# FOX projections of heads 0 to 3 as three Strassen chunks

## The chip, the cores and the metric

One core of a Trainium2 chip runs the kernel; the other cores are idle. The metric is the time of one execution in device microseconds (us), as the median of several runs. A core has a matrix engine (TensorE, PE in the profile, with its weight loads as PEld), a vector engine (VectorE, DVE), an activation engine (ScalarE, ACT), a general engine (GpSimd, POOL) and a queue that only issues transfers (SyncE, SP). They run side by side and wait for each other through semaphores; each works through its own queue in order.

## The reference

One decoder block on 512 tokens of width 1024, all in float32:

```python
u = rmsnorm(x, norm_mix_g)
proj = u @ w_in                      # 1024 x 9240
(gq, gk, gv, gz, ga, gb, fq, fk, fv, ff, gate_a, gate_b) = split(proj)
# A: conv(4) + SiLU on gq, gk, gv; gated delta rule, 8 heads of 128; norm * silu(gz)
y_a = o_a @ w_proj_gdn
# B (FOX): per head rmsnorm of q and k, softmax(q k^T / sqrt(128) + c_t - c_s), causal, 8 heads of 128
y_b = o_b @ w_proj_fox
h = x + (sigmoid(gate_a) * y_a + sigmoid(gate_b) * y_b) @ w_out
x = h + square(relu(rmsnorm(h, norm_mlp_g) @ w_up)) @ w_down
```

The change concerns `fq, fk, fv` of heads 0 to 3: twelve blocks of 128 columns of `w_in`, 1536 columns in all, multiplied by u (512 x 1024).

## The kernel before

**A product in three terms.** Matrices are split into a rounded part and a remainder (`hi`, `lo`). A product is hi·hi + lo·hi + hi·lo, so each 128 x 128 weight block costs three matmuls. The split is one ScalarE cast (hi) and one VectorE subtraction (lo); for weights that is `prefetch_split` (L256, L257), for activations `split` (L286, L287).

**Weights come in units.** The list `seq` names every unit of weights (128 x 1024, 512 KB) in the order of use. `unit(name)` takes the next one and, ahead of it, splits two further units (`LA_SPLIT`) and loads three (`LA_RAW`). There are four buffers for hi and four for lo (`whl`), three for raw weights (`wraw`) and two more for the first factor of a Strassen chunk (`swp`). SyncE issues plain loads (L210, L227). Since the planner (below) may run ahead, how early a unit is really loaded or split depends on these buffers.

**Strassen chunks.** `stream` computes 512 columns of a projection as a 2 x 2 block product with seven instead of eight half-sized products (the Winograd form): P1 to P7, each with its own weight unit and its own form of u. For P1, P2 and P3 a quarter of the weights is loaded as it is; the units of P5, P6, P4 and P7 are made in place, by a DMA that GpSimd issues and that adds another quarter onto the raw tile of an earlier product (L219): P1 → P5 → P6 → P4 and P3 → P7. Such a DMA must wait until the earlier unit has been split. Each product is 24 matmuls of 256 columns (L1011). P1, P6, P7 and P4 of a chunk follow each other in one PSUM bank (U), with an eviction after each (copies on ScalarE L991, additions and subtractions on VectorE L993); P5 and P3 share a second bank (V), P2 has a third (W). In all there are three such banks (`NMM`). Before the change, `STREAM` holds seven chunks: FOX heads 4 to 7 (three chunks) and the two gates (four).

**Forms of u.** P1, P2 and P4 use u itself. `factors_u` makes the others (P5, P7, P6, P3): in two parts it reloads the normalised x from DRAM (L432), scales it (L436), forms sums of half-width blocks (L448, two instructions a form) and splits the result (L286, L287). They stay in 16 pages until the stream ends.

**Pages.** Most activations live in 128 x 512 float32 pages, 53 in all (`NPG`). An instruction whose result has no free page cannot be placed.

**Order of the work.** The main program issues dense products; besides them run generators (`tasks`): one step of each at every `tick()`. The stages: norm of x and gates; z projections 0 to 4; `gdn_group(0)` with the 12 projections of delta-rule heads 0 to 3 (L275 to L279) and their head work; `fox_pair(0)` and `fox_pair(1)`, the FOX projections of heads 0 to 3 (L961 to L964), with `factors_u` started between them; z projections 5 to 7; `gdn_group(1)`; the stream of seven chunks; the output projections; the MLP in Strassen form (L1171). Generators beside them: `group_chain` (triangular inversion `invert`, then `scan` over four chunks of tokens), one and later two `fox_worker`s (attention of one head at a time, as soon as `fq` holds its q and k, and its v), `decays` (decay tables; those of group 1 start when group 0's chain has ended). In `invert`, 31 elimination steps of two VectorE instructions each give way to other tasks whenever their estimated work passes `INV_STEP[g]`.

**Planner.** The program is compiled with `schedule_with_timeline_sim=True`: a planner orders each engine's instructions by a simulated timeline and lets an instruction pass ahead of one whose inputs or buffers are not ready. The order of issue in the code is thus a priority, not the final order; the final order is fixed before the kernel runs.

**The old FOX stage.** `fox_pair` computes, for each of three panels and four token blocks, 256 columns with 24 matmuls (8 of uhi and 8 of ulo against the weights' hi, 8 of uhi against their lo): 2 x 3 x 4 x 24 = 576 matmuls.

Of the kernel before, what the change touches and what calls it, by code (L numbers as in the profile page):

```python
# [39 lines left out]
LA_SPLIT = 2  # L40
INV_STEP = (2500, 900)


def hybrid_block(tc, a, out):
# [106 lines left out]
    seq = [("w_ab", 0)] + [("w_z", i) for i in range(NZ1)]  # L151
    seq += [("w_gdn", i) for i in range(12)] + [("w_fox", i) for i in range(12)]
    seq += [("w_z", i) for i in range(NZ1, H)] + [("w_gdn", 12 + i) for i in range(12)]
# [46 lines left out]
    def load(n):  # L200
        nme, i = seq[n]
        if nme in FACTOR:
            w, c, s_ = i
            q, old = FACTOR[nme]
            if old is None:
                if w == "w_st":
                    raw = (swp if nme == "P1" else wraw).tile([P, D], F32, tag="raw", name=nm("sraw"))
                else:
                    raw = fresh[2 if nme == "P2" else s_].tile([P, D], F32, tag="raw", name=nm("draw"))
                nc.sync.dma_start(raw, a[w][c, q, s_])  # L210
            elif (nme, i) in LONE:
                if n not in begun:
                    begin(n)
                raw = begun[n]
                nc.gpsimd.dma_start(raw, a[w][c, 2, s_], accum_op=ALU.add)
            else:
                raw = factors[old, i]
                assert seq.index((old, i)) < len(units)
                nc.gpsimd.dma_start(raw, a[w][c, q, s_], accum_op=ALU.add)  # L219
            factors[nme, i] = raw  # L220
            raws[n] = raw, [slice(0, D)]
            return
        w = 256 if nme == "w_ab" else D
        raw = wraw.tile([P, D], F32, tag="raw", name=nm("raw"))
        cuts = [slice(0, 512), slice(512, D)] if 0 < n < 3 else [slice(0, w)]
        for c in cuts:
            nc.sync.dma_start(raw[:, c], a[nme][i][:, c])  # L227
        raws[n] = raw, cuts
# [6 lines left out]
    def prefetch_new(n):  # L235

        for m in range(pos[0], min(len(seq), n)):
            if fresh and m not in raws and seq[m][0] in FACTOR and FACTOR[seq[m][0]][1] is None and seq[m][1][0] != "w_st":
                load(m)
            if seq[m] in LONE and m not in begun:  # L240
                begin(m)
# [39 lines left out]

    def split(src, scale=None, dst=None):

        hi, lo = dst or (page(F32R, "hi")[:, :], page(F32R, "lo")[:, :])
        if scale is None:
            act.copy(hi, src)  # L286
            vec.tensor_tensor(lo, src, hi.bitcast(F32), op=ALU.subtract)  # L287
        else:
            act.activation(hi, src, AF.Copy, scale=scale)
            vec.scalar_tensor_tensor(lo, src, scale, hi.bitcast(F32),  # L290
                                     op0=ALU.mult, op1=ALU.subtract)
        return hi, lo
# [133 lines left out]
    def factors_u():  # L426
        lo, hi = slice(0, 256), slice(256, 512)
        for part in range(2):
# [9 lines left out]
            for p in ("P5", "P7", "P6", "P3"):  # L438
                yield
                x = s1 if p == "P5" else s2  # L440
                for f in range(2):
# [5 lines left out]
                                    "P3": (c[k + 4][:, lo], s2[:, o], ALU.add)}[p]  # L447
                    vec.tensor_tensor(x[:, o], in0, in1, op=op)  # L448
                xh_, xl_ = split(x)
                for f in range(2):  # L450
# [387 lines left out]

    def gdn_group(g, box):
        AT = atp.tile([P, NI, P], F32, tag="AT", name=nm("AT"))  # L840
        hd = drp.tile([5, NCH, P, G, P], F32, tag=f"hd{g}", name=f"hd{g}")
        hts = []
        for i in range(G):
            h = g * G + i
            ys = []
            for j in range(3):
                ys.append(project(h, j))
                tick()
            hts.append(start(head(h, AT, *ys, box, hd)))
        return start(group_chain(g, AT, hd, hts))  # L850

# [97 lines left out]

    def fox_pair(hp):  # L950
        vts = ([], [])
        for pn in range(3):
            us = [unit("w_fox"), unit("w_fox")]
            pg2 = [page(s="fqk"), page(s="fqk")]
            for t2 in range(2):
                ps = mmps("fx")
                for tb in (2 * t2, 2 * t2 + 1):
                    o = ps[:, (tb % 2) * 256:(tb % 2 + 1) * 256]
                    for k in range(KT):
                        w = us[k // 4][0][:, (k % 4) * 256:(k % 4 + 1) * 256]  # L960
                        mm(o, uhi[k][:, cs(tb)], w, start=(k == 0), stop=False)  # L961
                        mm(o, ulo[k][:, cs(tb)], w, start=False, stop=False)  # L962
                    for k in range(KT):
                        mm(o, uhi[k][:, cs(tb)], us[k // 4][1][:, (k % 4) * 256:(k % 4 + 1) * 256], start=False,  # L964
                           stop=(k == KT - 1))
                    if tb % 2 == 0:
                        tick()
                if pn < 2:
                    act.copy(pg2[t2], ps)
                else:  # L970
                    for j in range(2):
                        (vec.tensor_copy if j else act.copy)(
                            v3(pg2[j][:, 2 * t2 * P:(2 * t2 + 2) * P], 2), v3(ps[:, :], 2)[:, :, cs(j)])
                tick()
            if pn < 2:
                fq.append((2 * hp + pn, pg2, vts[pn]))
            else:
                for v, x in zip(vts, pg2):
                    v += [x[:, cs(c)] for c in range(NCH)]

    def stream(parts, other):

# [11 lines left out]

        for p, c in STREAM:
            if p is None:
# [16 lines left out]
            done = parts[c][2]  # L1013
            at[0] = c
            if p == "P1":
# [74 lines left out]
    fws = [start(fox_worker())]  # L1090
    ch0 = gdn_group(0, box)
    fox_pair(0)
    fu = start(factors_u())
    fox_pair(1)
    start(decays(1, box, ch0))
# [4 lines left out]
    hold[0] = False  # L1100
    finish(fu)
    fws += [start(fox_worker()) for _ in range(1, NFW)]
# [38 lines left out]
    parts += [gate_chunk(i, to) for to in (sga, mg) for i in range(2)]  # L1141
    stream(parts, merge_gdn)

# [296 lines left out]
def _layout(inputs):  # L1440
# [20 lines left out]
    fx = w[:, 4112:7184].reshape(D, 3, H, P)  # L1461
    pan = []
    for hp in range(2):
        for h in (2 * hp, 2 * hp + 1):
            pan.append(np.concatenate([fx[:, 0, h], fx[:, 1, h]], axis=1))
        pan.append(np.concatenate([fx[:, 2, 2 * hp], fx[:, 2, 2 * hp + 1]], axis=1))
    o["w_fox"] = c(np.stack(pan).reshape(6, 2, 4, P, 256).transpose(0, 1, 3, 2, 4).reshape(12, P, D))
    q, k, v = [[fx[:, j, h] for h in range(H)] for j in range(3)]
# [3 lines left out]

    st = np.stack(st).reshape(7, 2, 4, P, 2, 256)
    o["w_st"] = c(np.stack([st[:, j, :, :, l] for j, l in ((0, 0), (0, 1), (1, 1), (1, 0))], 1)
                  .transpose(0, 1, 3, 2, 4).reshape(7, 4, 1, P, D))
    o["w_z"] = units(w[:, 3072:4096])
# [43 lines left out]
```

## Time and profile before

| | |
|---|---|
| median of 3 runs | 983.23 us (983.08 to 983.75) |
| span of the profiled execution (first to last instruction) | 980.2 us |
| around the span (median less span) | 3.0 us |
| TensorE busy | 970.8 us, 6545 matmuls |
| VectorE / ScalarE / GpSimd busy | 710.9 / 605.0 / 240.2 us |
| first and last old FOX matmul | 122.4 and 213.2 us |
| first and last matmul of the stream (L1011) | 324.7 and 543.5 us |
| the chain that ended last | PE 92%, DVE 4%, DMA 2% |

The profiled execution has no time of its own other than its span; the 3.0 us lie around it. A page of the profile shows for each engine the time in which it was busy, the span cut into 40 equal slices, the chain of work that ended last and the costliest groups of instructions. A group's row ends with its busy time, the mean duration of one (ns), and the idle time of its engine just before, with what ended it. Matmuls are pipelined: the duration of one record is longer than the distance to the next.

### The profile page before, as it was taken

The numbers are of one execution on the slowest core, as the hardware profiler recorded it, in microseconds if no ns is written. First come the engines' busy times: TensorE is split into PE (matmuls) and PEld (weight loads), VectorE is DVE, ScalarE is ACT, GpSimd is POOL, SyncE is SP. The second block draws the span as 40 slices with busy tenths as digits, with TensorE's granted clock in tenths as the row PEclk, the third lists the DMA queues.
The fourth block names the chain that finished last, engine by engine and source line by source line (L and its number), as shares of the span: only waits on it lengthen the run. The fifth ranks groups of instructions, "written<-read, shape, count | busy, mean of one in ns | idle before, by whom it ended". The sixth has DMA issues, their size and how long they took to land.

```text
span 980.2 us, 17198 instructions
## 1 busy us (share of the span) xinstructions
PE 970.8 (99%) x6545; PEld 874.8 (89%) x6545; DVE 710.9 (73%) x1204; ACT 605.0 (62%) x1050; POOL 240.2 (25%) x236
## 2 busy tenths in 40 slices
PE   8999999999999999999999999999999999999998
PEld 6788899998888999999999888889989989988986
DVE  6877778566577789855656535889896697698596
ACT  7766444766564787867656422678755765666761
POOL 1544120202533513522320005312121121121110
PEclk9999999999999999999999999999999999999999
DMA  7647662475437885757887735688798888889884
GB/s 266 213 135 223 174 158 90 130 239 181 129 116 228 189 166 141 197 129 166 236 201 215 273 103 171 125 181 173 190 188 196 187 173 206 181 175 202 186 166 119
DMA packets 93442, 174.38 MB, mean 178 GB/s; under 512 B 8016, under 2 KB 49200, under 8 KB 93360
## 3 DMA queue, kind: packets, MB, share of 16 engines
q1 hardware_dynamic: 78928, 120.85, 38.8%
q0 software_dynamic: 14432, 52.44, 30.5%
q8 instruction: 51, 0.84, 0.4%
q14 instruction: 31, 0.25, 0.1%
HBM read 152.25 MB, written 21.02 MB: 177 GB/s over the span
## 4 chain that ended last, share of the span: by engine, by line
PE 92%; DVE 4%; DMA 2%; ACT 1%; issue 1%; SPq 0%; DVEq 0%
PE mlp L1171 36%; PE st L1011 12%; PE mm L279 8%; PE mm L276 8%; PE mm L275 8%; PE fx L964 2%; PE fx L961 2%; PE fx L962 2%; PE fo L944 2%; PE sc L919 1%; PE pT L935 1%; DVE lo L257 1%; PE kk L639 1%; PE kq L647 1%; DMA ux<-ud 1%; PE v L797 1%
## 5 line engine op out<-in xcount | busy, mean ns | idle before, releaser
L1402 ACT CAST hi<-draw 128x1024 fp32r<-128x1024 f32 x124 | 130.0, 1050 | 118.4 <-PE mlp L1171 100.4
L1409 DVE TENSOR_TENSOR lo<-draw,hi 128x1024 fp32r<-128x1024 f32 x124 | 151.3, 1222 | 44.8 <-ACT hi L1402 41.6
L256 ACT CAST hi<-raw 128x1024 fp32r<-128x1024 f32 (+1 forms) x62 | 62.9, 1021 | 82.6 <-PE mm L276 59.5
L1171 PE MATMUL mlp<-hi,shi 128*128 128x512 f32 x280 | 109.5, 391 | 0.1
L1171 PE MATMUL mlp<-hi,slo 128*128 128x512 f32 x280 | 109.1, 390 | 0.0
L1171 PE MATMUL mlp<-lo,shi 128*128 128x512 f32 x280 | 109.0, 389 | 0.0
L257 DVE TENSOR_TENSOR lo<-raw,hi 128x1024 fp32r<-128x1024 f32 (+1 forms) x62 | 73.9, 1197 | 29.1 <-ACT hi L256 13.4
L1171 PE MATMUL mlp<-shi,lo 128*128 128x256 f32 x448 | 90.3, 283 | 0.0
L1171 PE MATMUL mlp<-slo,hi 128*128 128x256 f32 x448 | 90.3, 283 | 0.0
L1171 PE MATMUL mlp<-shi,hi 128*128 128x256 f32 x448 | 90.3, 283 | 0.0
L276 PE MATMUL mm<-ulo,hi 128*128 128x512 f32 x216 | 85.0, 394 | 1.2 <-DVE ulo L290 1.2
L275 PE MATMUL mm<-uhi,hi 128*128 128x512 f32 x216 | 85.0, 395 | 0.0
L257 DVE TENSOR_TENSOR lo<-sraw,hi 128x1024 fp32r<-128x1024 f32 x49 | 60.7, 1240 | 20.9 <-ACT hi L256 20.1
L1171 PEld LDWEIGHTS mlp<-shi,hi 128*128 128x128 f32 x448 | 70.6, 192 | 0.9
L1171 PEld LDWEIGHTS mlp<-shi,lo 128*128 128x128 f32 x448 | 69.9, 192 | 0.0
L1171 PEld LDWEIGHTS mlp<-slo,hi 128*128 128x128 f32 x448 | 69.8, 192 | 0.0
L256 ACT CAST hi<-sraw 128x1024 fp32r<-128x1024 f32 x49 | 51.3, 1047 | 26.6 <-PE st L1011 16.2
L1171 PEld LDWEIGHTS mlp<-hi,shi 128*128 128x128 f32 x280 | 52.6, 188 | 11.1 <-issue 0.7
L1171 PEld LDWEIGHTS mlp<-lo,shi 128*128 128x128 f32 x280 | 52.6, 188 | 11.1
L1171 PEld LDWEIGHTS mlp<-hi,slo 128*128 128x128 f32 x280 | 52.6, 188 | 10.3
L219 POOL DMA_DIRECT2D draw<-w_d x30 | 26.3, 876 | 129.9 <-DVE lo L1409 120.8
L219 POOL DMA_DIRECT2D draw<-w_u x32 | 27.7, 866 | 122.6 <-DVE lo L1409 120.0
(336 smaller groups left out, 2466.6 us busy)
## 6 DMA issues: line engine op xcount, KB each, us to landing
draw<-w_u POOLq DMA_DIRECT2D x32, 512.0 KB, 5.7
draw<-w_d POOLq DMA_DIRECT2D x32, 512.0 KB, 6.5
sraw<-w_st POOLq DMA_DIRECT2D x28, 512.0 KB, 5.9
draw<-w_d SPq DMA_DIRECT2D x26, 512.0 KB, 4.4
raw<-w_gdn SPq DMA_DIRECT2D x24, 512.0 KB, 3.8
draw<-w_u SPq DMA_DIRECT2D x24, 512.0 KB, 4.4
sraw<-w_st SPq DMA_DIRECT2D x21, 512.0 KB, 5.5
hd<-hd SPq DMA_DIRECT2D x34, 256.0 KB, 5.4
```

Source lines behind the costliest of these rows:

```text
L219: nc.gpsimd.dma_start(raw, a[w][c, q, s_], accum_op=ALU.add)
L256: act.copy(hi[:, c], raw[:, c])
L257: vec.tensor_tensor(lo[:, c], raw[:, c], hi[:, c].bitcast(F32), op=ALU.subtract)
L275: mm(o, w, rhi(k), start=(k == 0), stop=False)
L276: mm(o, w, rlo(k), start=False, stop=False)
L279: mm(o, lo[:, k * cols:(k + 1) * cols], rhi(k), start=False, stop=(k == KT - 1))
L944: mm(po[:, cs(i)], vt[c], st[i][:, cs(c)], start=(c == 0), stop=(c == i))
L961: mm(o, uhi[k][:, cs(tb)], w, start=(k == 0), stop=False)
L1011: mm(o, u, w, start=first and t == 0 and k == 0 and j == 0 and x is hi, stop=x is lo and k == 3, skip_group_check=True)
L1171: return (lambda *args, **kw: tc.keep_in_program_order(f(*args, **kw))) if self.pinned[0] else f
L1402: pact.copy(hi, raws[m][0])
L1409: pvec.tensor_tensor(lo, raws[m][0], hi[:, :].bitcast(F32), op=ALU.subtract)
```

## The change

Heads 0 to 3 get the form that heads 4 to 7 have. `fox_pair` and its 12 units `w_fox` go; three Strassen chunks come in their place, with 21 units `w_sf` in an order of their own (`EARLY`), computed by the same `stream`, which now takes the order as an argument. Chunk 0 holds v0, v1, q0, k0; chunk 1 q2, k2, q1, k1; chunk 2 q3, k3, v2, v3. Since the products need all forms of u, `factors_u` now starts inside `gdn_group(0)`, after the projections of its second head, and is finished before the stream begins. Its sums, and the lo parts of its splits, are made by GpSimd instead of VectorE. `INV_STEP` for group 0 falls from 2500 to 1300.

```diff
-INV_STEP = (2500, 900)
+INV_STEP = (1300, 900)
...
-    seq += [("w_gdn", i) for i in range(12)] + [("w_fox", i) for i in range(12)]
+    seq += [("w_gdn", i) for i in range(12)]
+    EARLY = [("P1", 0), ("P2", 0), ("P1", 1), ("P2", 1), ("P5", 0), ("P3", 0), ("P6", 0), ("P5", 1), ("P7", 0), ("P4", 0),
+             ("P3", 1), ("P6", 1), ("P1", 2), ("P2", 2), ("P7", 1), ("P5", 2), ("P4", 1), ("P3", 2), ("P6", 2), ("P7", 2),
+             ("P4", 2)]
+    seq += [(p, ("w_sf", c, 0)) for p, c in EARLY]
...
-                if w == "w_st":
+                if w in ("w_st", "w_sf"):
                     raw = (swp if nme == "P1" else wraw).tile([P, D], F32, tag="raw", name=nm("sraw"))
...
-    def split(src, scale=None, dst=None):
+    def split(src, scale=None, dst=None, lo_by=None):
...
             act.copy(hi, src)
-            vec.tensor_tensor(lo, src, hi.bitcast(F32), op=ALU.subtract)
+            (lo_by or vec).tensor_tensor(lo, src, hi.bitcast(F32), op=ALU.subtract)
...
-                    vec.tensor_tensor(x[:, o], in0, in1, op=op)
-                xh_, xl_ = split(x)
+                    pool.tensor_tensor(x[:, o], in0, in1, op=op)
+                xh_, xl_ = split(x, lo_by=pool)
...
-    def gdn_group(g, box):
+    def gdn_group(g, box, between=None):
...
             hts.append(start(head(h, AT, *ys, box, hd)))
+            if between and i in between:
+                between[i]()
...
-    def fox_pair(hp):
...
-    def stream(parts, other):
+    def stream(parts, order, other=None):
...
-        for p, c in STREAM:
+        for p, c in order:
...
-            at[0] = c
+            if other:
+                at[0] = c
...
-    ch0 = gdn_group(0, box)
-    fox_pair(0)
-    fu = start(factors_u())
-    fox_pair(1)
+    fu = []
+    ch0 = gdn_group(0, box, {1: lambda: fu.append(start(factors_u()))})
+    finish(*fu)
+    v01, v23 = ([], []), ([], [])
+    stream([fox_chunk((None, v01), (0, v01[0])), fox_chunk((2, v23[0]), (1, v01[1])), fox_chunk((3, v23[1]), (None, v23))],
+           EARLY)
     start(decays(1, box, ch0))
...
     ch1 = gdn_group(1, box)
     hold[0] = False
-    finish(fu)
...
-    stream(parts, merge_gdn)
+    stream(parts, STREAM, merge_gdn)
```

On the host side the quarters of `w_sf` are laid out as those of `w_st` are.

More of the change, by code (lines that the diff above doesn't have):

```diff
@@ L237, in prefetch_new @@
         for m in range(pos[0], min(len(seq), n)):
-            if fresh and m not in raws and seq[m][0] in FACTOR and FACTOR[seq[m][0]][1] is None and seq[m][1][0] != "w_st":
+            if fresh and m not in raws and seq[m][0] in FACTOR and FACTOR[seq[m][0]][1] is None and seq[m][1][0] not in ("w_st", "w_sf"):
                 load(m)
@@ L948, in fox_worker @@
             stores.append(start(store_late(obd[h], o)))
-    def fox_pair(hp):
[L951 to L979, printed above, removed]
-    def stream(parts, other):
+    def stream(parts, order, other=None):
         bank = {}
@@ L1461, in _layout @@
     fx = w[:, 4112:7184].reshape(D, 3, H, P)
[L1462 to L1467, printed above, removed]
     q, k, v = [[fx[:, j, h] for h in range(H)] for j in range(3)]
@@ L1471, in _layout @@
     st += [w[:, n + T * i:n + T * i + T] for n in (7192, 8216) for i in range(2)]
-    st = np.stack(st).reshape(7, 2, 4, P, 2, 256)
-    o["w_st"] = c(np.stack([st[:, j, :, :, l] for j, l in ((0, 0), (0, 1), (1, 1), (1, 0))], 1)
-                  .transpose(0, 1, 3, 2, 4).reshape(7, 4, 1, P, D))
+    sf = [np.concatenate(b, axis=1) for b in
+          ((v[0], v[1], q[0], k[0]), (q[2], k[2], q[1], k[1]), (q[3], k[3], v[2], v[3]))]
+    for name, m in (("w_sf", sf), ("w_st", st)):
+        m = np.stack(m).reshape(len(m), 2, 4, P, 2, 256)
+        o[name] = c(np.stack([m[:, j, :, :, l] for j, l in ((0, 0), (0, 1), (1, 1), (1, 0))], 1)
+                    .transpose(0, 1, 3, 2, 4).reshape(len(m), 4, 1, P, D))
     o["w_z"] = units(w[:, 3072:4096])
```

## The prediction

> **What bounds the kernel now.** I read the profile page first: totals, the slices and the granted clock.
>
> ```profile
> span 980.2 us, 17198 instructions
> ...
> PE 970.8 (99%) x6545; PEld 874.8 (89%) x6545; DVE 710.9 (73%) x1204; ACT 605.0 (62%) x1050; POOL 240.2 (25%) x236
> ...
> PE   8999999999999999999999999999999999999998
> ...
> PEclk9999999999999999999999999999999999999999
> ```
>
> TensorE is busy in every slice at full clock. Next I asked the waits for TensorE alone: is that busy time work, or work stretched by stalls?
>
> ```profile
> PE mm L276 <- DVE ulo L290: 1.2, 2, 0.7
> ...
> PE Q L741 <- ACT AT L725: 0.5, 1, 0.5
> ...
> PE pT L935 <- DVE p L932: 0.2, 1, 0.2
> ```
>
> The first is the largest, the last the smallest of nine kinds; they are 5.5 us together. So no other engine sets the end. Time leaves this kernel if TensorE has fewer matmuls to issue, and comes back if something makes TensorE wait.
>
> The busy time by stretches shows what other engines have to spare. The first row is the projections of delta-rule heads 0 to 3, the second the FOX projections that are replaced, the third the first part of the existing Strassen stream.
>
> ```profile
> 43.00:122.00 79.00, 77.79 (x385) 64.60 (x384) 63.29 (x127) 47.26 (x103) 26.45 (x22) 1.00 0.60 174
> ...
> 122.40:213.40 91.00, 90.52 (x926) 88.63 (x925) 60.00 (x147) 52.10 (x104) 14.26 (x13) 1.00 0.51 151
> 324.70:420.00 95.30, 95.13 (x818) 91.93 (x818) 81.58 (x196) 75.73 (x161) 37.21 (x35) 1.00 0.77 176
> ```
>
> After the length: busy time of PE, PEld, DVE, ACT, POOL; then clock, DMA share, GB/s. The third row matters most: there a Strassen stream already runs beside a delta-rule inversion, with DVE at 86%, ACT at 79% and DMA at 0.77, and TensorE still lost only 0.17 us of 95.3.
>
> **Part 1: fewer matmuls.** The groups of TensorE by line and their timeline (several merged into a row):
>
> ```profile
> L961 PE MATMUL fx<-hi,uhi 128*128 128x256 f32 x192 | 48.5, 288 | 0.0
> L962 PE MATMUL fx<-hi,ulo 128*128 128x256 f32 x192 | 47.8, 284 | 0.0
> ...
> L964 PE MATMUL fx<-lo,uhi 128*128 128x256 f32 x192 | 28.4, 285 | 0.0
> ```
> ```profile
> 124.28 1.12 PE L964 MATMUL fx<-lo,uhi 128*128 128x256 f32 x8
> ...
> 342.79 0.64 PE L1011 MATMUL st<-lo,hi 128*128 128x256 f32 x4
> ...
> 346.68 1.06 PE L647 MATMUL kq<-conv,conv 128*128 128x128 f32 x8
> 347.57 0.60 PE L919 MATMUL sc<-fk,fq 128*128 128x256 f32 x2
> 347.82 0.59 PE L1011 MATMUL st<-lo,hi 128*128 128x256 f32 x2
> ```
>
> Removed: 3 x 192 = 576 matmuls of 256 columns. Added: 3 chunks x 7 products x 2 halves x 12 = 504 of the same shape. The existing stream confirms the count: its own matmuls, alone, are these.
>
> ```profile
> 324.70:543.60 218.90, 156.87 (x1176) 145.81 (x1175) 1.00 0.75 184
> ```
>
> 1176 / 7 chunks = 168 a chunk, and 3 x 168 = 504. So 72 fewer. One record lasts 285 ns, but they overlap: eight take 1.12 us, so (1.12 - 0.28) / 7 = 0.120 us from one to the next; four of the stream take 0.64, again (0.64 - 0.28) / 3 = 0.120. The saving is 72 x 0.120 = **8.6 us**, not 72 x 0.285 = 20.5. All other matmuls stay; the stage shrinks from 91.0 to about 82.4 us, and a unit of weights (24 matmuls) lasts 2.9 us of pure stream, or 82.4 / 21 = 3.9 us with the other tasks' matmuls between.
>
> **Part 2: the weights.** 12 units become 21: 9 plain loads by SyncE, 12 adding DMAs by GpSimd, each onto the raw tile that the unit before it in its chain has just been split from. Rows of the replaced stretch, and one eviction of the stream (L993):
>
> ```profile
> L257 DVE TENSOR_TENSOR lo<-raw,hi 128x1024 fp32r<-128x1024 f32 x12 | 14.5, 1218 | 6.1 <-PE fx L964 4.1 <-ACT hi L256 1.3 <-issue 0.8
> ...
> L287 DVE TENSOR_TENSOR lo<-ux,hi 128x512 fp32r<-128x512 f32 x4 | 3.6, 896 | 1.8 <-ACT hi L286 1.8
> ...
> L448 DVE TENSOR_TENSOR ux<-ux,ux 128x256 f32<-128x256 f32 x6 | 2.3, 423 | 0.1
> ...
> L448 DVE TENSOR_TENSOR ux<-ux 128x256 f32<-128x256 f32 x2 | 1.2, 633 | 0.0
> ```
> ```profile
> L993 DVE TENSOR_TENSOR fqk<-fqk,st 128x512 f32<-128x512 f32 x9 | 6.1, 676 | 1.8 <-ACT fqk L991 1.8
> ```
> ```profile
> L256 ACT CAST hi<-raw 128x1024 fp32r<-128x1024 f32 x11 | 11.3, 1049 | 14.7 <-PE fx L962 14.7
> L436 ACT ACTIVATE ux<-ux,c_norm_mix_g 128x512 f32<-128x512 f32 x8 | 5.5, 723 | 2.7 <-DMA ux<-ud 2.6
> L969 ACT COPY fqk<-fx 128x512 f32<-128x512 f32 x8 | 4.6, 580 | 3.3 <-PE fx L964 3.3
> ```
>
> DVE in the stage: 60.0, plus 9 splits x 1.22 = 11.0, plus 9 subtracting or adding evictions x 0.68 = 6.1, less the sums of u that leave (3.6 + 2.3 + 1.2): 70.0 of 82.4 us, 85%. ACT: 52.1 + 9 x 1.05 + 4 more copies x 0.58 - 5.5 for u's scalings = 58.4, 71%. Both are below the third stretch's 86% and 79%, where TensorE did not wait. DMA, from the queues' rows and the landings:
>
> ```profile
> q1 hardware_dynamic: 78928, 120.85, 38.8%
> q0 software_dynamic: 14432, 52.44, 30.5%
> ```
> ```profile
> sraw<-w_st POOLq DMA_DIRECT2D x28, 512.0 KB, 5.9
> ```
> ```profile
> DMA to landing us min/median/max: 3.4/5.7/10.4
> ```
>
> A 512 KB (0.524 MB) adding transfer occupies the 16 engines for 0.305 x 980.2 x 0.524 / 52.44 = 2.99 us, a plain one for 0.388 x 980.2 x 0.524 / 120.85 = 1.65. The stage has 0.51 x 91 = 46.4 us; plus 12 x 2.99, less 3 x 1.65, less the reloads of u (8 half-sized, 6.6) gives 70.7 of 82.4, a share of 0.86 against 0.77: the one resource above its precedent. A link of a chain is a split (1.05 + 1.22) and a landing (5.9): 8.2 us. Split buffers are four, so unit n can be split once unit n-4 is used. In the new order the tightest links are two units long (P5 to P6 of chunk 0; P6 to P4 and P3 to P7 of chunk 2): P5 is split from 2.9 us on, P6 is then ready at 2.9 + 2.3 + 5.9 + 2.3 = 13.4 us, and wanted at 6 x 2.88 = 17.3. Spare 3.9 us; with the longest landing, 10.4, it would be 0.6 late. Cost taken: nothing, hidden behind the four units between; without that cover up to 0.6 us plus what DVE has queued ahead, at three links. GpSimd's queue gets 12 issues, each waiting for DVE's lo; behind one stand the FOX normalisations and the delta-rule output scaling, whose own results go to pages that the stream does not read.
>
> **Part 3: banks handed over without a unit between.** Products 6, 7 and 4 share one PSUM bank, and each must wait until the one before is evicted. In the new order P7 and P4 of chunk 0, and P6, P7, P4 of chunk 2, stand next to each other; the existing order always puts a unit between. From both sides: 0 each if the planner fills in other work (346.68 to 347.82 above shows it running kq and sc inside a unit), or a tail of 0.16, an eviction of 0.68 and one split ahead of it, 1.22: 2.1 each, 6.2 in all. Another chunk's unit, or the z projection behind, is ready at each place, so I take **1.0**, near the lower end.
>
> **Part 4: sums of u by GpSimd, earlier.** 16 sums of 128x256 and 8 differences of 128x512, with their 8 reloads, 8 scalings and 8 casts, move into the second half of the first group. The nearest GpSimd rows of these shapes:
>
> ```profile
> L1229 POOL TENSOR_TENSOR m<-gate,gate 128x256 f32<-128x256 f32 x16 | 19.6, 1241 | 83.2 <-DVE gate L1227 83.2
> ...
> L573 POOL TENSOR_TENSOR gu<-upper,ghi 128x512 fp32r<-128x512 f32 x8 | 9.4, 1176 | 12.0 <-ACT ghi L507 12.0
> ```
>
> 19.6 + 9.4 = 29.0 us, so GpSimd goes from 26.5 to 55.5 of 79. Their casts on ACT, and DVE's differences as they are now (min/median/max):
>
> ```profile
> L286 ACT CAST hi<-ux x8: 603/618/622, 193.0 to 237.5; 128x512 fp32r<-128x512 f32 x8
> L287 DVE TENSOR_TENSOR lo<-ux,hi x8: 681/688/1528, 193.6 to 238.2; 128x512 fp32r<-128x512 f32 x8
> ```
>
> In series a form takes 2 x 1.24 + 0.62 + 1.18 = 4.3 us, eight 34 us. From the middle of the group (82.5), with 5.5 for a reload and 2.9 for scalings: 125; with half of GpSimd's own 26.5 us between them, 138. The last form (P3) is wanted by unit 5, at 122.4 + 14.4 + some 3 us of other matmuls = 140. Just in time, so I charge nothing; each us beyond is a us of TensorE idle.
>
> GpSimd and DVE do hold each other up in this trace:
>
> ```profile
> 193.60 1.53 DVE L287 TENSOR_TENSOR lo<-ux,hi 128x512 fp32r<-128x512 f32 x1 [1.12 <-ACT hi L286]
> ```
> ```profile
> 192.54 2.04 POOL L889 TENSOR_TENSOR fqk<-fqk,fss 128x512 f32<-128x512 f32 x2
> 194.53 1.09 POOL L878 TENSOR_SCALAR_AFFINE_SELECT nd<-row 128x512 f32<-128x512 f32 x1
> ```
>
> The difference took 1.53 us instead of the median 0.69, with GpSimd's two multiplications from 192.54 to 194.58 beside it: it began 1.06 us after them, and its end, 195.13, comes 0.55 after theirs. If GpSimd's 29 us were all added to DVE, it would have 63.3 + 29 = 92 us of work in 79. But in that half of the group DVE has only 6 or 7 such two-input instructions of size, the weight splits; each waiting one GpSimd instruction of 1.2 makes 8 us, against 79 - 63.3 = 15.7 idle in the whole group, some 8 in this half. TensorE meanwhile has two more projection banks to fill, each 24 matmuls, by this row (1.98 - 0.39) / 7 = 0.227 us apart, 5.5 us:
>
> ```profile
> 50.24 1.98 PE L279 MATMUL mm<-uhi,lo 128*128 128x512 f32 x8
> ```
>
> Cost taken 0; bound 1.5 (one GpSimd instruction and some).
>
> [...]
>
> **Part 5: inversion steps.** By the code's count the 31 steps give way 9 times instead of 5, and the stage ticks 21 times, not 24, so group 0's chain ends 7 ticks later against group 1, and the decay tables with it. Heads 4 and 5 wait for theirs; the group's chain starts only after head 7, which has its table some 9 ticks early. Cost 0; if that cover went, one projection, 5.5 us, at most.
>
> **Sum.** 980.2 - 8.6 + 1.0 = 972.6 us of span. The run's median is 983.2, 3.0 more than the span; kept, that gives **975.6**. Its own range: 973.5 (no handover cost, the 0.5 wait at L741 gone, 0.6 for parts that this cannot see) to 978.5.
>
> **Rivals.** (a) *The weights come late.* For: DMA at 0.86, links of two units. Three links late by 0.6 + 1.2, or 5.4 us: **981.0**. Against: 85% of DVE has a precedent without waits, and several units are split ahead. (b) *GpSimd and DVE hold each other up; slower than before.* The place is the wait of unit 4 or 5 on the forms, its price the lateness one to one; it decides from 8.6 - 1.0 = 7.6 us on, and is measurably slower from about 9.6. If the two engines' lock stretches GpSimd's 29 us by half, 14.5 us, the last form is at 152, 12 late: **987.6**. (Seen from DVE, 92 - 79 = 13 us: nearly the same.) For: the 256-wide row of GpSimd, 1.24, is longer than the 512-wide one, 1.18, so it was stretched by something. Against: it takes half of GpSimd's other work ahead of the sums, and both parts strictly in series. [...] (c) *Pages run out.* u's 16 factor pages are taken from about 100 us on instead of from 193 to 238. In the new stage I count 32 for u and forms, 8 to 12 for FOX results, 5 of head 3, 5 of the inversion, 3 of the worker: 53 to 57 of 53. A chunk that cannot be evicted stops TensorE until pages return. Stopped for half of a chunk, 3.5 units x 3.9 = 14 us: **989.6**. Against: the third stretch holds the 32 and 12 too, with a head's and an inversion's pages and two workers', and shows 95.13 of 95.30. (d) *The change does nothing*, since something else sets the end: **983**. Against: 5.5 us of waits in 980.
>
> **Chances.** Forecast 0.68; (a) 0.14, of which 0.05 lands within 0.2%; (b) 0.09 (0.02 faster, 0.02 same, 0.05 slower); (c) 0.06 (0.01, 0.01, 0.04); (d) 0.03, same. Faster 0.68 + 0.09 + 0.02 + 0.01 = 0.80; same 0.11; slower 0.09. 0.2% (2.0 us) is about what a measurement of this kernel can tell from no change. The range runs from 973.5 to 982.0, through (a) and the 6.2 us handover bound; outside lie most of (b) and (c).
>
> **What would show it.** Right: the stream's line with 1680 matmuls at the same 0.12 us spacing, TensorE's busy time and span both lower by about 8 us, the total of its waits still below 8. (a) shows as TensorE waiting for lo splits whose casts wait for adding DMAs; (b) as one wait early in the stage on a GpSimd lo; (c) as TensorE waiting for evictions that sit idle themselves. Wrong altogether: a span that stays although 72 matmuls are gone.

## The result, and the profile after

The changed kernel takes **1009.46 us** (median of 4 runs, 1006.91 to 1010.19) against 983.37 for the kernel before (4 runs, 983.08 to 983.75) on the same chip: a ratio of 1.026, 95% interval 1.0242 to 1.0279. It is 26 us slower where 8 us less were forecast. The profiled run took 1010.19 us, 1.7 more than its span.

The page of the kernel after: totals, slices and granted clock.

```profile
span 1008.5 us, 17125 instructions
...
PE 974.1 (97%) x6473; PEld 873.6 (87%) x6473; DVE 720.2 (71%) x1194; ACT 616.8 (61%) x1061; POOL 274.3 (27%) x272
...
PE   8999979899999599999999999999999999999998
...
PEclk9999999999999799999999999999999999999999
```

The matmuls fell by 72, from 6545 to 6473, and yet TensorE is busy for 3.3 us more. There are new holes in its slices and one in its clock, all before 355 us. Next, the busy time by stretches, cut at the first matmul of the new stage and at the start of the later stream; first the kernel before, then the kernel after (length; busy PE, PEld, DVE, ACT, POOL; clock, DMA share, GB/s):

```profile
122.40:324.70 202.30, 201.82 (x1525) 183.25 (x1524) 135.75 (x299) 116.38 (x236) 53.37 (x46) 1.00 0.53 158
324.70:980.30 655.60, 651.05 (x4457) 595.17 (x4455) 479.75 (x732) 408.77 (x661) 144.96 (x146) 1.00 0.76 180
```
```profile
122.75:346.60 223.85, 200.84 (x1452) 179.77 (x1452) 141.47 (x288) 121.08 (x235) 69.50 (x65) 0.96 0.58 155
346.60:1008.60 662.00, 655.61 (x4456) 597.88 (x4456) 483.19 (x738) 409.88 (x663) 146.39 (x148) 0.99 0.76 178
```

Up to 122 us next to nothing is lost (0.35 us). In the next stretch TensorE has 73 matmul records fewer and needs 21.6 us more; it idles 23.0 us of it instead of 0.5. The rest, the same work in both, is 6.4 us longer. So the loss lies around the new stage and the second delta-rule group, and it is waiting. The waits of TensorE in the kernel after (us in total, times, longest):

```profile
PE st L986 <- DVE conv L603: 13.7, 3, 10.2
PE st L986 <- ACT fqk L966: 2.9, 3, 1.1
PE Qp L711 <- DVE Xd L693: 2.6, 1, 2.6
PE st L986 <- DVE fqk L968: 1.3, 3, 0.8
```

The timeline of the kernel after shows where they lie (start, duration, then in brackets the idle time before and what ended it). Two undisturbed rows of the stream stand on top.

```profile
123.77 0.64 PE L986 MATMUL st<-lo,uhi 128*128 128x256 f32 x4
124.25 0.64 PE L986 MATMUL st<-hi,uhi 128*128 128x256 f32 x4
...
132.72 0.71 PE L986 MATMUL st<-hi,uhi 128*128 128x256 f32 x4 [3.11 <-DVE conv L603]
...
142.80 0.71 PE L986 MATMUL st<-hi,uhi 128*128 128x256 f32 x4 [0.38 <-DVE fqk L968]
...
146.69 0.74 PE L986 MATMUL st<-hi,hi 128*128 128x256 f32 x4 [0.78 <-DVE fqk L968]
...
150.97 0.75 PE L986 MATMUL st<-hi,hi 128*128 128x256 f32 x4 [1.15 <-ACT fqk L966]
...
155.25 0.74 PE L986 MATMUL st<-hi,hi 128*128 128x256 f32 x4 [1.15 <-ACT fqk L966]
...
196.72 1.20 PE L711 MATMUL Qp<-Xd,AT 32*32 32x32 f32 x64 [2.56 <-DVE Xd L693]
...
346.64 1.19 PE L986 MATMUL st<-hi,uhi 128*128 128x256 f32 x4 [10.16 <-DVE conv L603]
```

Four matmuls every 0.48 us: 0.120 each, as forecast. Most of what is new are three larger waits (3.1, 2.6 and 10.2 us) and four handovers. A second cost is the **granted clock**. In the kernel before it was full in every slice; these are stretches of the kernel after, and two rows of the stream out of the first:

```profile
134.00:137.00 3.00, 3.00 (x16) 3.00 (x15) 0.96 (x5) 0.57 (x1) 2.09 (x3) 0.50 0.61 74
199.00:202.00 3.00, 3.00 (x16) 3.00 (x16) 0.16 (x1) 2.92 (x6) 0.00 (x0) 0.50 0.87 248
271.00:273.50 2.50, 2.50 (x13) 2.50 (x12) 2.01 (x3) 1.76 (x3) 2.50 (x3) 0.50 0.31 92
348.00:351.00 3.00, 3.00 (x16) 3.00 (x15) 2.96 (x8) 1.36 (x3) 0.39 (x1) 0.50 0.86 147
```
```profile
135.34 1.05 PE L986 MATMUL st<-hi,ulo 128*128 128x256 f32 x4
136.20 1.05 PE L986 MATMUL st<-lo,uhi 128*128 128x256 f32 x4
```

Four matmuls of the stream take 0.86 us at clock 0.50 (135.34 to 136.20), 0.48 at full clock: 44% of such a stretch is lost. In the trace the clock is halved in 133.9 to 137.3, 198.7 to 202.2, 270.4 to 273.8 and 338.7 to 352.3 us. The first three follow shortly on waits and are 3.4, 3.5 and 3.4 us long; the fourth begins in the wait of 10.2 us and is 13.6 long. TensorE works in 3.4, 3.5, 3.4 and (after its wait ends at 346.6) 5.7 us of them, 16 us in all, and 44% of it is about 7 us lost, an estimate (the matmuls of 270.4 to 273.8 are of other sizes). The last section sets the waits before them beside these lengths.

The account of the span: 72 x 0.120 = 8.6 us less work; waits of all kinds 24.6 more (30.1 against 5.5, adding up the waits of TensorE); clock about 7; sum 23 of the 28.3 us. The other 5 I can't assign.

### The profile page after: what moved, and what is told of

It is laid out like the page before. It is cut to its first block, busy times and chain, and to the rows that moved or that the text cites. A ratio compares the mean times of both kernels' runs of the same rounds, so it can differ in the third digit from the quotient of the medians.

```text
span 1008.5 us, 17125 instructions
## 1 busy us (share of the span) xinstructions
PE 974.1 (97%) x6473; PEld 873.6 (87%) x6473; DVE 720.2 (71%) x1194; ACT 616.8 (61%) x1061; POOL 274.3 (27%) x272
## 4 chain that ended last, share of the span: by engine, by line
PE 74%; DVE 9%; DMA 8%; ACT 4%; issue 3%; POOL 1%; SPq 1%; POOLq 0%; DVEq 0%; ACTq 0%
PE mlp L1148 35%; PE st L986 12%; PE mm L283 6%; PE mm L279 6%; PE mm L280 6%; DMA row<-rowd 2%; DVE lo L261 2%; PE fo L950 1%; DMA sraw<-w_sf 1%; ACT hi L260 1%; DMA sraw<-w_st 1%; DMA row<-oad 1%; DVE conv L603 1%; PE sc L925 1%; DMA ux<-ud 1%
## 5 line engine op out<-in xcount | busy, mean ns | idle before, releaser
L261 DVE TENSOR_TENSOR lo<-sraw,hi 128x1024 fp32r<-128x1024 f32 x70 | 88.1, 1259 | 39.1 <-ACT hi L260 37.8
L260 ACT CAST hi<-sraw 128x1024 fp32r<-128x1024 f32 x70 | 73.3, 1048 | 65.9 <-PE st L986 28.8
L260 ACT CAST hi<-raw 128x1024 fp32r<-128x1024 f32 (+1 forms) x50 | 50.4, 1014 | 62.8 <-PE mm L280 50.8
L261 DVE TENSOR_TENSOR lo<-raw,hi 128x1024 fp32r<-128x1024 f32 (+1 forms) x50 | 59.6, 1195 | 34.0 <-ACT hi L260 18.6
```

The lines of the kernel that those rows point to most:

```text
L260: act.copy(hi[:, c], raw[:, c])
L261: vec.tensor_tensor(lo[:, c], raw[:, c], hi[:, c].bitcast(F32), op=ALU.subtract)
```

## The experiments

Ratios are to the kernel before, run beside the edited one on the same chip (medians 981.65 to 982.9), with 95% intervals. Differences of microseconds between two runs are taken between what each of them lies above the kernel before on its own chip. INV_STEP is 1300 in the change and was 2500. The theories are numbered in the expectations in the order in which they came up. Those that matter most: T1, the spread inversion makes group 0's chain late; T2, GpSimd's sums hold VectorE up; T4, chunk 2's adding DMAs come late; T5, the two raw tiles of a chunk's first factors are too few; T6, the forms of u, on whatever engine, make the end of group 0 late; T7, the row tiles of the decay tables are too few; T8, the chains of splits and adding DMAs set the pace; T9, VectorE has too much to do beside the elimination.

### One part undone at a time

**The inversion as before**, the rest as changed:

```diff
-INV_STEP = (1300, 900)
+INV_STEP = (2500, 900)
```

> The changed kernel with group 0's inversion steps as before (2500). Theory T1, the inversion: spread over 47 us (148 to 195) instead of some 26, it makes group 0's chain late, the decay tables of group 1 late, and so the 10.2 us wait of TensorE before the stream; then this kernel loses that wait and its half-clock time, and comes to 985 to 995 us. Theory T2, the GpSimd sums: nothing much changes, 1005 to 1010 us. Theory T3, the chunks themselves (weights and handovers of banks): 1005 to 1010 us.

Measured 999.03 us, 1.0178 (1.0149 to 1.0208), 17.0 us above the kernel before: about 9 us of the 26 are the spreading. The wait of 10.2 us before the later stream is gone. But `Qp`, the first matmul of the delta-rule chain after the elimination, now waits 7.0 us instead of 2.6.

**The sums of u on VectorE again**, the rest as changed:

```diff
-                    pool.tensor_tensor(x[:, o], in0, in1, op=op)
-                xh_, xl_ = split(x, lo_by=pool)
+                    vec.tensor_tensor(x[:, o], in0, in1, op=op)
+                xh_, xl_ = split(x)
```

> The changed kernel with the sums of u and their lo parts on VectorE again, still made in the first group. T2, the GpSimd sums: the 3.1 us wait at 129.6 and what follows from it go, 985 to 1000 us. T1, the inversion: the wait before the stream stays, 1000 to 1010 us. T3, the chunks: 1003 to 1010 us.

1011.17 us, 1.0302 (1.0272 to 1.0332): not better. The wait at 129.6 us, 3.1 in the kernel after, is 4.5 here. T2 falls. That GpSimd helps isn't shown either: the next run and the one with the old inversion differ in this alone and agree within 0.2 us.

**Both undone** (the two edits above together), so that only the three chunks are left, with the early start of the forms that they need:

> The three chunks alone: sums on VectorE (still in the first group) and the inversion steps at 2500. T1 or T2 or both together: everything comes back but the chunks' own saving, 974 to 982 us. T3, the chunks: still slower than before, 990 us or more, with waits of TensorE on evictions inside the early stream.

999.19 us, 1.018 (1.015 to 1.021), with `Qp` waiting 8.1 us. So the chunks, with the forms of u made early for them, lose 17 us by themselves where they were to save 8.6.

**The spreading alone**, on the kernel before:

```diff
-INV_STEP = (2500, 900)
+INV_STEP = (1300, 900)
```

> The kernel before with the inversion steps of group 0 at 1300, nothing else. T1, the inversion: the chain comes late here too, 988 to 1005 us. T2 and T3: 983 us, no difference.

984.34 us (8 runs), 1.0025 (1.0013 to 1.0037), one new wait of 1.5 us. Spreading costs 2 us without the chunks, about 9 with them; T1, which had 988 us or more here, misses. One reason can be read from the trace: without the chunks the planner hardly spreads the elimination, whose last step starts at 171.7 us instead of 170.3.

### Why the spreading costs 9 us

In the kernel after, the elimination ends at 195.3 us (170.3 before) and group 1's decay tables, which follow the chain of group 0, come late. The timeline of the kernel after around the 10.2 us wait:

```profile
323.45 1.84 POOL L592 TENSOR_TENSOR eb<-em,row 128x512 f32<-128x512 f32 x1 [7.24 <-DMA row<-rowd]
331.61 1.29 POOL L592 TENSOR_TENSOR eb<-em,row 128x512 f32<-128x512 f32 x1 [5.06 <-DMA row<-rowd]
332.84 0.91 POOL L223 DMA_DIRECT2D sraw<-w_st  x1
...
343.53 1.04 ACT L260 CAST hi<-sraw 128x1024 fp32r<-128x1024 f32 x1 [17.18 <-DMA sraw<-w_st]
344.49 0.68 ACT L600 ACTIVATE conv<-mm,c_conv 128x512 f32<-128x512 f32 x1
```

GpSimd makes the tables one at a time, each waiting for a row tile from DRAM; of the three row tiles two belong to the FOX worker. Behind the last table stands, in GpSimd's queue, the adding DMA of a weight. It is issued at 332.84 and has landed when ScalarE's cast starts at 343.53, 10.7 us later (the median of these transfers is 7.2). Behind that cast, in ScalarE's queue, stands the eviction of the last projection (L600), and TensorE waits for its bank: three queues, each in order, hand one lateness on. **A fourth row tile**, with INV_STEP at 1300 as changed, takes away the first link alone:

```diff
-    rwp = mix.enter_context(tc.tile_pool(name="rwp", bufs=3))
+    rwp = mix.enter_context(tc.tile_pool(name="rwp", bufs=4))
```

> The changed kernel (inversion steps 1300) with four instead of three buffers for row tiles. Theory T7, the 10.2 us before the stream is row tiles fetched one after another through the one buffer that the FOX worker leaves free, which turns the late decay tables into a late end of group 1: with one more buffer the wait falls under 4 us, 997 to 1002 us. Rival, lateness of group 0's chain alone sets it: the wait stays near 10 us, 1006 to 1010 us.

996.23 us (992.27 and 1000.20), 1.014 (1.0036 to 1.0243): 11.5 us back by the median, but the two executions lie 8 us apart. The trace is of the slower one, and there the 10.2 us wait is 1.7. T7 holds for the wait; how much time it is worth is known only roughly.

### Why the chunks alone lose 17 us

From here on INV_STEP is 2500, so the comparison is with 999.03. First the elimination in the kernel before, first and last instruction, and the `Qp` that follows:

```profile
143.49 0.91 DVE L681 TENSOR_TENSOR tmp<-E,X 128x31 f32<-128x31 f32 x1
...
170.27 0.17 DVE L683 TENSOR_TENSOR X<-X,tmp 128x16 f32<-128x16 f32 x1
174.95 1.20 PE L707 MATMUL Qp<-Xd,AT 32*32 32x32 f32 x64
```

And in the changed kernel with the inversion as before, with what stands around the last steps:

```profile
149.23 0.21 DVE L685 TENSOR_TENSOR tmp<-E,X 128x31 f32<-128x31 f32 x1
...
179.68 1.22 DVE L261 TENSOR_TENSOR lo<-sraw,hi 128x1024 fp32r<-128x1024 f32 x1
181.21 0.88 POOL L223 DMA_DIRECT2D sraw<-w_sf  x1 [5.82 <-DVE X L687]
...
185.00 0.21 DVE L687 TENSOR_TENSOR X<-X,tmp 128x45 f32<-128x45 f32 x1
187.60 1.04 ACT L260 CAST hi<-sraw 128x1024 fp32r<-128x1024 f32 x1 [5.26 <-DMA sraw<-w_sf]
188.68 1.22 DVE L261 TENSOR_TENSOR lo<-sraw,hi 128x1024 fp32r<-128x1024 f32 x1 [3.47 <-ACT hi L260]
189.82 0.18 DVE L685 TENSOR_TENSOR tmp<-E,X 128x30 f32<-128x30 f32 x1
...
190.47 0.17 DVE L687 TENSOR_TENSOR X<-X,tmp 128x16 f32<-128x16 f32 x1
191.87 1.92 PE L711 MATMUL Qp<-Xd,AT 32*32 32x32 f32 x64 [6.95 <-DVE Xd L693]
```

The elimination starts 5.7 us later, takes 41.4 us instead of 27.0 and ends 20.2 late. Between 185.2 and 189.8 its last steps stand in VectorE's queue behind a weight's subtraction, which waits for a cast, which waits for an adding DMA, which was issued only after the unit before had been split (179.68; the profile names the elimination step that ended just behind that split). `Qp` stands in TensorE's queue ahead of the last five units of the stream; the order is fixed, so these wait with it. TensorE reaches `Qp` at 184.9 us and starts it at 191.9, 16.9 us later than in the kernel before. Then it works at half clock: the stretches 196 to 203 us of this run and of the one below without the elimination.

```profile
196.00:203.00 7.00, 6.74 (x115) 5.97 (x116) 3.04 (x8) 4.39 (x12) 0.00 (x0) 0.50 0.15 40
```
```profile
196.00:203.00 7.00, 6.91 (x65) 6.71 (x66) 1.96 (x3) 3.61 (x6) 4.60 (x4) 1.00 0.48 177
```

How full is VectorE meanwhile? The stretch 142 to 176 us, in the kernel before and in the changed one with the old inversion:

```profile
142.00:176.00 34.00, 34.00 (x341) 33.87 (x339) 27.64 (x78) 15.51 (x24) 2.87 (x4) 1.00 0.34 96
```
```profile
142.00:176.00 34.00, 30.55 (x249) 29.77 (x248) 30.30 (x64) 18.58 (x27) 10.14 (x11) 1.00 0.77 176
```

81% with the whole elimination in it, against 89% with some 20 of the 31 steps, by the groups of these two stretches: ten weights are split there instead of six. From the first to the last step the trace tells how the 14.4 us come about by which the elimination grew. In the kernel before VectorE is busy for 22.0 of 27.0 us, with 4 weight splits between the steps; here for 33.9 of 41.4 us, with 11. So 11.9 us of the 14.4 are more work in its queue, and 2.5 are more idle time, with the one wait of 3.5 us behind the adding DMA in it.

**Without group 0's elimination** (its 62 instructions are left out, five breaks stay):

```diff
-        for j in range(B - 1):
+        for _ in range(5 if rest == INV_STEP[0] else 0):
+            yield
+        for j in range(0 if rest == INV_STEP[0] else B - 1):
```

> Inversion steps at 2500; the 62 VectorE instructions of group 0's elimination are left out, its five breaks kept (the inverse of the diagonal blocks is then the identity; group 1 keeps its own). Theory T9, VectorE's load in the stretch from 142 on is what TensorE waits for: without those 16.5 us the wait at Qp near 185 goes, below 1 us, and 984 to 990 us against 999. Rival T8, the weights' transfers set it: the wait stays above 4 us, 994 to 999 us.

985.68 us (8 runs), 1.0041 (1.003 to 1.0052): 13.6 us back, and `Qp` doesn't wait. In the kernel before nothing of TensorE's 5.5 us of waits is at `Qp`, so there the elimination has next to nothing to give back. The 13.6 us fit the trace with the elimination: 7.0 us of wait, and some 4.5 us for the 10.6 us of work in the half clock that follows until 204 us (44%, an estimate). TensorE's busy time, and the largest waits left:

```profile
PE 965.8 (98%) x6473; PEld 868.5 (88%) x6473; DVE 703.3 (72%) x1132; ACT 614.5 (63%) x1059; POOL 276.2 (28%) x272
```
```profile
PE st L988 <- DVE conv L603: 3.1, 1, 3.1
PE st L988 <- ACT fqk L968: 2.3, 2, 1.1
PE st L988 <- DVE fqk L970: 1.6, 2, 0.8
```

So the meeting of the stream's splits with the elimination on VectorE costs most of the 17 us. That the wait ends when the elimination is gone doesn't say why it was late; the next runs take other things off VectorE and off the chain.

**Every second split of the new units on GpSimd**:

```diff
+            i = seq[len(units)][1]
+            by = pool if type(i) is tuple and i[0] == "w_sf" and len(units) % 2 else vec
-                vec.tensor_tensor(lo[:, c], raw[:, c], hi[:, c].bitcast(F32), op=ALU.subtract)
+                by.tensor_tensor(lo[:, c], raw[:, c], hi[:, c].bitcast(F32), op=ALU.subtract)
```

> Inversion steps at 2500; the lo part of every second weight unit of the new stream is made by GpSimd instead of VectorE, the whole computation is kept. T9: VectorE is rid of some 12 us and the wait at Qp falls from 7 to under 3 us, 986 to 993 us. Rivals: GpSimd holds VectorE up as much as it takes from it, or its slower splits make the adding transfers later (T8): 996 to 1004 us.

1001.62 us, 1.0189 (1.0127 to 1.025), within the rivals' range and not T9's. `Qp` waits 2.5 instead of 7.0, but this doesn't speak for T9: TensorE comes to `Qp` 7.4 us later (192.3 instead of 184.9), after waits of 9.2 and 4.0, and the elimination itself ends 3 us later than in the run with the old inversion. The wait at 129 us grows from 3.1 to 9.2. GpSimd is busy for 15.0 of the 17 us from 122 on, and VectorE's convolution steps stand behind a 128 x 4 instruction that takes 3.50 us beside it.

**Plain loads instead of the adding DMAs** (each unit loads its own quarter; the 12 additions are left out):

```diff
+            elif w == "w_sf":
+                raw = wraw.tile([P, D], F32, tag="raw", name=nm("sraw"))
+                nc.sync.dma_start(raw, a[w][c, q, s_])
```

> Inversion steps at 2500; the additions are left out of the 12 adding transfers of the new stream: each is a plain load by SyncE into a tile of its own (the FOX products of heads 0 to 3 are then of other weights; splits and matmuls stay the same). Theory T8, the chains split, adding DMA, split set the pace at the end of the new stream and VectorE stands behind the late splits: the 7 us wait near 185 goes with its half-clock stretch, 986 to 991 us against 999. Rival T9, VectorE is late for its load alone (splits, evictions, inversion): the wait stays above 4 us, 995 to 1000 us.

992.85 us, 1.0107 (1.0072 to 1.0142): 7 us back, `Qp` waits 4.0. The chain of adding DMAs is a part of the cost, not all of it: the result lies between T8's range and T9's, and the elimination still takes 39 us instead of 27.

**No forms of u** (the products use u's own blocks; reloads, scalings, sums and splits are left out), and then **both left out**, by this edit and the one above:

```diff
-    ch0 = gdn_group(0, box, {1: lambda: fu.append(start(factors_u()))})
+    for k in range(4):
+        for p in ("P5", "P7", "P6", "P3"):
+            uforms[p, k] = uforms["P1", k]
+    ch0 = gdn_group(0, box)
```

> Inversion steps at 2500; the forms of u for P5, P7, P6 and P3 are left out (no reload, scaling, sums or splits; those products use u's own blocks), in the early stream and in the later one. T6, the forms' work in group 0 makes VectorE late for the last projection's bank: the 3.1 us wait at 129 goes, and 990 to 995 us. Rival, the first splits of the stream do: it stays, 997 to 1000 us.

> Both left out, the additions of the new stream's transfers and the forms of u. If T6 and T8 name all there is beside the inversion and the bank handovers (three waits of 0.8 to 1.1 us): 976 to 981 us, below the kernel before. If something else of the chunks costs more (T9): 984 us or more.

1005.20 us, 1.0233 (1.0203 to 1.0262), and 1001.21 us, 1.0192 (1.0146 to 1.0237). The wait at 129 us is gone in both, so T6 is right about that wait, though not about the time. Yet each is slower than the run that differs from it in keeping the forms: `Qp` waits 13.6 and 8.4 us, since the stream reaches it sooner (at 176 us instead of 185), and new waits of up to 5.1 us come up in group 1.

### Other orders and buffers

**The forms a head earlier**, a **third raw tile** for first factors (paid with a page), and **another order** (P3 of chunk 1 between P7 and P4 of chunk 0, two z projections between the last three products), each by itself:

```diff
-    ch0 = gdn_group(0, box, {1: lambda: fu.append(start(factors_u()))})
+    ch0 = gdn_group(0, box, {0: lambda: fu.append(start(factors_u()))})
```

```diff
-NPG = 53
+NPG = 52
-    swp = mix.enter_context(tc.tile_pool(name="swp", bufs=2))
+    swp = mix.enter_context(tc.tile_pool(name="swp", bufs=3))
```

```diff
-    ("P7", 0), ("P4", 0), ("P3", 1), ("P6", 1), …, ("P6", 2), ("P7", 2), ("P4", 2)]
+    ("P7", 0), ("P3", 1), ("P4", 0), ("P6", 1), …, ("P6", 2), (None, NZ1), ("P7", 2), (None, NZ1 + 1), ("P4", 2)]
```

> Inversion steps at 2500, and the forms of u started after the first head of group 0 instead of the second. Theory T6, the 3.1 us wait at 129 (the third bank, held by the last projection's convolution) comes from VectorE and GpSimd being loaded with forms at the group's end: with the forms a head earlier it falls under 1.5 us, and 993 to 997 us. Rival, VectorE is late there by the stream's own first splits: the wait stays, 998 to 1000 us.

> Inversion steps at 2500 and three instead of two buffers for the first factor of a chunk (one page of 53 is given up for the room). Theory T5, chunk 2 starts late since its first tile waits for chunk 0's last split: with a third buffer its chain runs ahead and the 7 us wait near 185 goes, 985 to 992 us. Rival T4, the pace of links (split, DMA, split) and the four hi/lo buffers hold it: 996 to 1001 us, the wait stays.

> Inversion steps at 2500 as in the run that gave 999 us, and another order: P3 of chunk 1 between P7 and P4 of chunk 0, and z projections 5 and 6 between the last three products. Theory T4, TensorE starves at the end of the new stream because chunk 2's adding DMAs come late and nothing else stands in its queue: with two projections of 5.5 us there, the 7 us wait near 185 shrinks to under 2 us and its half-clock stretch goes, 985 to 991 us. Rival, the chunk is late whatever stands between, and the wait only moves: 996 to 1001 us.

1021.86 us, 1.04 (1.0357 to 1.0443): the 129 us wait moves to 95 and 108 us and becomes 3.5 and 5.8, `Qp` waits 13.7, and group 1 has new waits of 5.1, 1.1 and 3.2. 997.31, 1.015 (1.01 to 1.0201): `Qp` still waits 7.7, T5 falls. 995.28, 1.013 (1.0087 to 1.0173): other work ahead of `Qp` cuts its wait to 4.1, where T4 had less than 2.

**Several together**: the old inversion, four row tiles, the existing stream's order and z projections in the tail; then tail, row tiles and splits on GpSimd; then, as a floor, four row tiles with elimination and forms left out:

> A candidate that keeps the whole computation: inversion steps at 2500, four row buffers, the order of the existing stream for the new one (a unit between P2, P5 and P3 too), and z projections 5 and 6 between its last products. If the waits named so far are the cause: the 1.1 us waits near 150 go, the one near 185 stays at some 4 us, 986 to 993 us. If the forms come too late for a P5 in third place: one wait of 3 to 8 us near 130 in their place, 994 to 1000 us.

> A candidate with the whole computation: inversion steps at 2500, four row buffers, z projections 5 and 6 between the last products, every second lo part by GpSimd. If T9 holds and the parts add up: 984 to 990 us; not faster than the kernel before, since the 3.1 us wait at 129 and the three handovers of about 1 us stay. If they do not add up: 992 to 1000 us.

> Inversion steps at 2500, four row buffers; group 0's elimination and all forms of u left out. If the saving of 72 matmuls is real and only VectorE's work in the way of it: 976 to 982 us, with TensorE's waits under 6 us beside those of the kernel before. If the chunks cost by something else still: 985 us or more.

1000.19, 1.0181 (1.0152 to 1.0211), with waits of 3.1, 3.9, 2.5 and 5.5 us; 1001.87, 1.0191 (1.0162 to 1.0221), with 9.2 and 5.4; 998.16, 1.0154 (1.0124 to 1.0183). The gains don't add. The last was forecast lowest and is 12 us above the run that leaves out less: it waits 10.6 us in three places of group 1 for projections' evictions and 4.6 us in group 0's chain (`Q`). Each edit also makes the planner order everything anew, so a single edit's effect holds some us that are not the edit's own. None of these beats the kernel before.

## Why the prediction was wrong, point by point

**Part 1, fewer matmuls: right.** The stream's groups by line count 1680 in all (three of each of these sizes, 3 x 560), 0.120 us apart at full clock. No run brought the 8.6 us into the span; the nearest to it is the run without the elimination, where TensorE is busy for 965.8 us instead of 970.8.

```profile
L986 PE MATMUL st<-hi,hi 128*128 128x256 f32 x320 | 56.6, 294 | 4.0 <-ACT fqk L966 2.9 <-DVE fqk L968 0.9
...
L986 PE MATMUL st<-hi,uhi 128*128 128x256 f32 x144 | 25.6, 300 | 14.1 <-DVE conv L603 13.7 <-DVE fqk L968 0.4
...
L986 PE MATMUL st<-uhi,hi 128*128 128x256 f32 x96 | 15.9, 287 | 0.0
```

**Part 2, the weights: the step that failed.** "70.0 of 82.4 us, 85%" is an average over the stage, and the precedent at 86% has seven chunks' time to even out (my reading, not tested). The new units are pure stream at 2.9 us at first, and their splits fall into the 34 us in which the elimination must end, where VectorE was at 81% already. I asked whether the stream would wait for VectorE; it hardly does. What waits is the delta-rule chain, and then TensorE for it. "Cost taken: nothing" was 13.6 us by the run without the elimination, with the half clock after the wait in it.

**Part 3, the handovers: right that banks cost waits, wrong in place and size.** "I take 1.0" for three places; measured 0.38 + 0.78 + 1.15 + 1.15 = 3.5 us at four others, each below the 2.1 bound. By the matmuls before them they lie at the fifth to eighth product that TensorE takes up. Where the prediction looked, TensorE waits once, 0.6 us ahead of the last three products. I had counted neighbours in bank U alone; the new order starts two chunks at once on three banks, and the two waits of 1.15 us are behind ScalarE's copies (L966).

**Part 4, the sums: too low.** TensorE doesn't wait for GpSimd's forms, but for the last projection's bank, 3.1 us, twice the "bound 1.5". GpSimd holding VectorE up is in it. VectorE's timeline in the kernel after, and GpSimd's beside it:

```profile
129.33 1.81 DVE L621 TENSOR_SCALAR ssk<-ssk 128x4 f32<-128x4 f32 x1
129.41 1.70 POOL L452 TENSOR_TENSOR ux<-ux,ux 128x256 f32<-128x256 f32 x2
131.06 1.52 DVE L603 SCALAR_TENSOR_TENSOR conv<-mm,c_conv,conv 128x510 f32<-128x510 f32 x2
```

A tiny VectorE instruction of 1.81 us ends with GpSimd's two sums (at 131.14 and 131.11), and the two convolution steps for which TensorE waits come behind it. With the sums on VectorE itself this instruction takes 0.16 us and the wait is longer still, so GpSimd alone isn't the cause; the forms' work is: without it the wait is gone, and a head earlier it moved along.

**Part 5, the inversion: the second step that failed.** "Cost 0; if that cover went, one projection, 5.5 us, at most." It cost about 9 us with the chunks and 2 without. The lateness went through row tiles, an adding DMA and a cast to an eviction, none of which the step named; "at most one projection" assumed that the last projection itself would be the thing delayed, when what was delayed was the queue ahead of its eviction.

**A term left out: the clock.** No wait was priced with the half clock after it, about 7 us here. The trace of before shows none: its clock is full in every slice, and its longest wait was 1.1 us, ahead of its first matmuls.

**The rivals.** (a), late weights: a part of the truth, 7 us by the run with plain loads, but at the inversion and not in the stream. (b), GpSimd and VectorE holding each other up: fell as the cause of the slowdown, which is the same with the sums on VectorE (999.19 against 999.03). (c), pages: tested only in passing, by the run with a page fewer, which wasn't slower (997.31 against 999.03); the 10.2 us wait has other links, shown above. (d) fell: the change did something. The "3.0 around the span" was high too: it set the span of one execution against the median of others. It is 1.7 in the run after and in executions of the kernel before (982.33 with a span of 980.6).

**Open.** Why group 1 gets new waits (5.1, 1.1 and 3.2 us, or nearly these) in four runs. They aren't due to leaving something out: the run with the forms a head earlier has them and keeps the whole computation. In all four traces, ahead of the first wait, the evictions of two finished projections stand in ScalarE's queue behind the copy of a result of the delta-rule scan, which waits for TensorE (without the forms, the copy at 272.45 and the evictions at 272.93 us); in the run with the old inversion only one eviction stands there. Why the planner puts them so isn't shown. Open too is how the 13.6 us divide: the trace above puts most of the elimination's delay down to VectorE's work, but the one run that moved work of the splits to GpSimd did not shorten the time.

## What to carry to other kernels

When one engine at 99% is relieved, cost the change by the stretch in which the next engine meets its hardest deadline, not by its average over the stage, and ask of every instruction on it what stands behind it in its queue and who waits for that. A cover of "other work is ready" holds only if that work stands ahead in a queue whose order is already fixed. Price an isolated wait of some 3 us on TensorE at its length and about 1.5 us for each 3.4 us of half clock behind it (44% of 3.4, an estimate from the stream's rows above): one such stretch followed the 3.1 us wait in the kernel after; in the run with the old inversion, whose clock is 0.91 over 122.7 to 160.0, about twice as much followed it.

## What the runs showed of the hardware

The half clock came here behind waits of different lengths: that at 133.9 follows a wait of 3.1 us, that at 198.7 waits of 2.6 and 0.6, that at 270.4 waits of 1.1 and 0.7, and that at 338.7 comes 2.2 us into the wait of 10.2. The four handovers of 0.4 to 1.15 us, some 4 us apart, brought none: the clock is 1.00 from 142 to 166. What length or sequence of waits brings it isn't shown.

A VectorE instruction on 128 x 4 elements with one tensor as input took 1.81 us beside GpSimd's sums, and 0.16 where VectorE made the sums itself; in the kernel before all eight executions of this instruction took 0.16 to 0.17. The line's eight executions in the kernel after (min/median/max in ns):

```profile
L621 DVE TENSOR_SCALAR ssk<-ssk x8: 165/254/1812, 75.6 to 355.1; 128x4 f32<-128x4 f32 x8
```

I had counted only the large two-input instructions as exposed to GpSimd. No trace had shown that limit, and this row speaks against it.
